# Reading the token operand of a matmul as two halves in turns, and moving the phases of its operands

## The chip, the cores and the metric

The kernel runs on one core of one Trainium2 chip. A core has five engines with instruction streams of their own (TensorE for matmuls, VectorE, ScalarE, GpSimd, SyncE), an on-chip memory of 128 partitions (SBUF), an accumulator memory for matmul outputs (PSUM) and DMA queues to the device memory. The metric is the device time of one execution in microseconds. Before the change it is 2859.04 us, the median of three runs (2858.79 to 2860.81).

In the profile PE is TensorE's matmul stream, PEld its weight loads, DVE is VectorE, ACT is ScalarE, POOL is GpSimd and SP is SyncE. A name like L184 is a line of the kernel's file.

## What is computed

One layer of a decoder over 280 tokens: 16 learned meta tokens, 256 prompt tokens and 8 sample tokens, with a model width of 2048 and an inner width of 5504, all in fp32:

```python
x = layer_norm(ALPHA * x + 0.5 * swiglu(x, f1_g, f1_u, f1_d), ln1_g, ln1_b)
m, s_ret, s_hg = token_mixer(x, ...)     # 10 projections of x, two recurrences, w_out
x = layer_norm(ALPHA * x + m, ln2_g, ln2_b)
x = layer_norm(ALPHA * x + 0.5 * swiglu(x, f2_g, f2_u, f2_d), ln3_g, ln3_b)

def swiglu(x, w_gate, w_up, w_down):
    return (jax.nn.silu(x @ w_gate) * (x @ w_up)) @ w_down
```

Outputs are the tokens without the meta tokens and the recurrent states. Each weight matrix is read once; nearly all arithmetic is in the dense products.

## The kernel before

**Layout.** Features lie on partitions, tokens along the free axis. The 2048 features are 16 tiles of 128 (`KC`), the inner 5504 are 43 (`FC`). A dense product is a sequence of matmuls with a 128x128 weight block as stationary operand and one token tile of 280 columns (264 from the output gate on: the meta tokens are dropped) as moving operand.

**Two parts for each number.** Weights and tokens are split into a high and a low part (`whi`, `wlo`; `xh`, `xl`; `hh`, `hl` for the inner activations; `yh`, `yl` for the mixer's output). Each block takes three matmuls into the same PSUM bank: high by high (L183), high weights by low tokens (L184), low weights by high tokens (L185). These three lines, in `dense`, are nearly all of TensorE's work. Each matmul has its own weight load, which overlaps the matmul before it.

**Order of the dense work.** The up product (names `up...`) goes by 22 groups of two inner tiles, gate and up for each, so four output banks: for each of the 16 token tiles `k`, four blocks in turn, hence 16 x 4 x 3 = 192 matmuls a group (96 in the last). The down product (`dn...`) goes by 16 output tiles, each summed over 43 inner tiles, one bank at a time. The mixer (`pj_...`) projects in groups of two with 16 token tiles each, and between its matmuls, by `pump`, the recurrences run as generators. The output projection (`wo`) follows. The first group of the mixer and of the second up product is made by `Norm.first`, from token tiles (`xhg`, `xlg`) that have not been normalised yet and are two columns wider; then `Norm.normalise` writes the final tiles. TensorE's order is the order of the program; the other engines' work is ordered by the scheduler, with weight loading at high priority.

**Weight feed.** `stream` loads 8 blocks (a unit, 512 KB) by one DMA from SyncE's queue into `raw` (three buffers). ScalarE casts it to `whi` (L157) and VectorE subtracts to get `wlo` (L158), three buffers each. A unit feeds 24 matmuls.

**Where the operands lie.** SBUF addresses are bytes within a partition. `raw` has a pitch of 512 bytes per block; `whi` and `wlo` are padded to `WP` = 132 columns per block, a pitch of 528 bytes, so successive blocks start 16 bytes further modulo 512, and a buffer is 4224 bytes. The token tiles `xh` and `xl` are separate tiles of `XP` = 296 columns (1184 bytes) of which a window of 280 or 264 is used; `x_tiles` shifts its start by 0 to 12 columns by the tile's number. `hh` and `hl` are tiles of exactly 280 or 264 columns (1120 or 1056 bytes).

Of the kernel before, what the change touches and what calls it, by code (L numbers as in the profile page):

```python
# [11 lines left out]
F32R = mybir.dt.float32r  # L12
# [6 lines left out]
P = 128  # L19
D = 2048  # L20
KC = D // P
DFF = 5504
FC = DFF // P
NMETA, SEQ, NS = 16, 256, 8
LP = NMETA + SEQ
T = LP + NS
# [5 lines left out]
U = 8  # L32


WP = P + 4
XP = 296

WARM = 7

# [14 lines left out]
def ffn_up_groups():  # L54
    g = []
    for m in range(0, FC, 2):
        ms = list(range(m, min(m + 2, FC)))
        g.append([("g", x) for x in ms] + [("u", x) for x in ms])
    return g
# [42 lines left out]
def trunk(ctx: ExitStack, tc: tile.TileContext, A, O):  # L102
    nc = tc.nc
    cst = ctx.enter_context(tc.tile_pool(name="cst", bufs=1))
    xp = ctx.enter_context(tc.tile_pool(name="xp", bufs=1))
    rp = ctx.enter_context(tc.tile_pool(name="rp", bufs=1))
    wp = ctx.enter_context(tc.tile_pool(name="wp", bufs=3))
# [5 lines left out]
    def acc_bank(name):  # L113
        return ps_a.tile([P, 512], F32, tag="acc", name=name)
# [25 lines left out]
    def turn(n):  # L140

        return tc.high_priority(offset=tc.tile_snap_priority() + 100 * (9 - n))

    def stream(w_dram, at_once=False):

        n_units = w_dram.shape[0]
        state = {"u": -1, "j": U, "hi": None, "lo": None}

        def load(u, parts=((0, U, tc.high_priority),)):
            raw = wp.tile([P, U, P], F32, tag="raw", name=f"raw{u}", bufs=3)  # L150
            hi = wp.tile([P, U, WP], F32R, tag="whi", name=f"whi{u}")[:, :, :P]
            lo = wp.tile([P, U, WP], F32R, tag="wlo", name=f"wlo{u}")[:, :, :P]
            src = w_dram[u].rearrange("p (b c) -> p b c", b=U)
            for j0, j1, when in parts:
                with when():
                    nc.sync.dma_start(raw[:, j0:j1, :], src[:, j0:j1, :])
                    nc.scalar.copy(hi[:, j0:j1, :], raw[:, j0:j1, :])  # L157
                    nc.vector.tensor_tensor(out=lo[:, j0:j1, :], in0=raw[:, j0:j1, :], in1=hi[:, j0:j1, :].bitcast(F32), op=ALU.subtract)  # L158
            return hi, lo

        def block():
            if state["j"] == U:
                state["u"] += 1
                assert state["u"] < n_units
                state["hi"], state["lo"] = load(state["u"])
                state["j"] = 0
            j = state["j"]
            state["j"] += 1
            return state["hi"][:, j, :], state["lo"][:, j, :]

        if at_once:
            state["hi"], state["lo"] = load(0, ((0, 2, lambda: turn(1)), (2, U, lambda: turn(2))))
            state["u"] = state["j"] = 0
        return block

    def dense(block, nk, outs, xhi, xlo, cols=slice(0, T), hook=None):
        n = len(outs)
        for k in range(nk):
            for i in range(n):
                wh, wl = block()  # L180
                h, l = xhi[k][:, cols], xlo[k][:, cols]
                o = outs[i][:, : h.shape[1]]
                nc.tensor.matmul(o, wh, h, start=k == 0, stop=False)  # L183
                nc.tensor.matmul(o, wh, l, start=False, stop=False)  # L184
                nc.tensor.matmul(o, wl, h, start=False, stop=k == nk - 1)  # L185
            if hook is not None:
                hook(k)

    def split(hi, lo, x):
        nc.scalar.copy(hi, x)  # L190
        nc.vector.tensor_tensor(out=lo, in0=x, in1=hi.bitcast(F32), op=ALU.subtract)  # L191
# [6 lines left out]
    def mul(out, a, b):  # L198
        nc.vector.tensor_tensor(out=out, in0=a, in1=b, op=ALU.mult)
# [20 lines left out]
    xh = [None] * KC  # L220
    xl = [None] * KC

    def x_tiles(c, which, n=T):
        for e, (x, nm) in enumerate(((xh, "xh"), (xl, "xl"))):
            o = 4 * ((2 * c + e) // 8 % 2) + 8 * (c % 2) * e
            x[c] = xp.tile([P, XP], F32R, tag=f"{nm}{c}", name=f"{nm}{which}_{c}")[:, o : o + n]

    def row_tile(name, n=T):
        return rp.tile([P, n], F32, tag=name, name=name)
# [1 line left out]
    class Norm:  # L231
# [57 lines left out]
        def shifted(self, m):  # L289
            n, d = self.n, self.d[m]  # L290
            if m == 0:
                nc.scalar.copy(self.s1, d)
                nc.scalar.activation(self.s2, d, AF.Square)
            else:
                self.q = q = self.row("lnq")
                nc.scalar.activation(q, d, AF.Square)
                if m == KC - 1 and not self.lead:
                    return
                add(self.s1, self.s1, d)
                add(self.s2, self.s2, q)  # L300
            if self.lead:
                x_tiles(m, f"g{self.which}", n + 2)
                g = self.g[:, m : m + 1]
                dx = self.dx[m][:, : n + 1]
                nc.scalar.activation(xh[m][:, : n + 1], dx, AF.Identity, scale=g)
                nc.vector.scalar_tensor_tensor(
                    out=xl[m][:, : n + 1], in0=dx, scalar=g, in1=xh[m][:, : n + 1].bitcast(F32), op0=ALU.mult, op1=ALU.subtract)
                nc.vector.tensor_copy(xh[m][:, n + 1 : n + 2], self.bs[:, 0, m : m + 1])
                nc.vector.tensor_copy(xl[m][:, n + 1 : n + 2], self.bs[:, 1, m : m + 1])
# [34 lines left out]
        def normalise(self):  # L344
            for c in range(KC):
                d = self.d[c]
                g, b = self.g[:, c : c + 1], self.b[:, c : c + 1]
                sub(d, d, self.mean)
                nc.vector.scalar_tensor_tensor(out=d, in0=d, scalar=g, in1=self.r, op0=ALU.mult, op1=ALU.mult)
                x_tiles(c, self.which, self.n)  # L350
                nc.scalar.activation(xh[c], d, AF.Identity, bias=b)  # L351
                nc.vector.scalar_tensor_tensor(  # L352
                    out=xl[c], in0=d, scalar=b, in1=xh[c].bitcast(F32), op0=ALU.add, op1=ALU.subtract)
# [37 lines left out]
    def ffn(i, block, w_dn, which, before=None):  # L391

        n = T if before is None else TL
        cols = slice(0, n)
        with tc.tile_pool(name=f"h{i}", bufs=1) as hp:
            hh, hl = [None] * FC, [None] * FC
            for gn, grp in enumerate(ffn_up_groups()):
                bank = acc_bank if gn % 2 == 0 else mx_bank
                outs = [bank(f"up{gn}_{j}") for j in range(len(grp))]
                if gn == 0 and before is not None:  # L400
                    outs = before.first(block, outs)
                else:
                    dense(block, KC, outs, xh, xl, cols)
                ng = len(grp) // 2
                for j in range(ng):
                    m = grp[j][1]
                    sg = hp.tile([P, n], F32, tag="sg", name=f"sg{m}", bufs=2)
                    nc.scalar.activation(sg, outs[j][:, :n], AF.Silu)
                    mul(sg, sg, outs[ng + j][:, :n])
                    hh[m] = hp.tile([P, n], F32R, tag=f"hh{m}", name=f"hh{m}")  # L410
                    hl[m] = hp.tile([P, n], F32R, tag=f"hl{m}", name=f"hl{m}")
                    split(hh[m], hl[m], sg)
            if before is not None:

                warm = hp.tile([P, 1], F32, tag="warm", name="warm")
                nc.scalar.activation(warm, sg[:, 0:1], AF.Abs_reciprocal_sqrt, scale=0.0, bias=eps_l)
            block = stream(w_dn)
            norm = Norm(which, n, False, i == 1)
            for m in range(KC):
                o = acc_bank(f"dn{m}")  # L420
                norm.ahead(m)
                dense(block, FC, [o], hh, hl, cols, (lambda k: k == 6 and norm.shift()) if m == 1 else None)
                norm.chunk(m, o[:, :n])
        return norm


    with tc.tile_pool(name="inp", bufs=2) as ip:
# [11 lines left out]
        up1 = stream(A["w_up1"], at_once=True)  # L439
# [19 lines left out]
    nc.sync.dma_start(sel, A["sel"])  # L459

    norm1 = ffn(1, up1, A["w_dn1"], 1)


    with tc.tile_pool(name="yp", bufs=1) as yp:
        yh, yl = [None] * KC, [None] * KC
        with tc.tile_pool(name="mp", bufs=1) as mp:
# [25 lines left out]
            nc.sync.dma_start(sin, A["sin"])  # L492

            block = stream(A["w_in"])
            st = {}
            on_r, on_h = {}, {}
# [375 lines left out]
        block = stream(A["w_out"])  # L872
        norm2 = Norm(2, TL, True, True)
        for gn, grp in enumerate(out_groups()):
            outs = [acc_bank(f"wo{m}") for m in grp]
# [4 lines left out]


    norm3 = ffn(2, stream(A["w_up2"]), A["w_dn2"], 3, norm2)
    norm3.finish(O["y"])

# [111 lines left out]
```

## Time and profile before

| | value |
|---|---|
| median of three runs | 2859.04 us |
| the profiled execution's span, first to last instruction | 2857.5 us |
| TensorE matmul (PE) busy | 2829.5 us, 99% |
| TensorE weight load (PEld) busy | 2775.9 us, 97% |
| VectorE busy | 1688.2 us, 59% |
| ScalarE busy | 1328.4 us, 46% |
| granted TensorE clock, mean | 0.999 |
| DMA | 186 GB/s from and to device memory over the span |

The profile shows of the profiled execution its span; no other time of it is given, and the runs' median lies 1.5 us above that span. The dense stages follow one another: first up product until about 543 us, first down product until about 809 us, the mixer until about 1993 us, the output projection until about 2087 us, second up product until about 2588 us, second down product until about 2841 us, then the last normalisation and the output.

How to read the rows: in the rows of groups, "x" is a count; after the bar stand busy time, mean duration of one, and the idle time of the engine before them with what ended it. Rows of one tile's instructions have shortest, median and longest duration in ns, then the first and last start in us. Matmuls are pipelined: a matmul's duration is longer than the distance to the next one's start, so the pace is busy time by count, or the distance between starts.

### The profile page before, as it was taken

The numbers are of one execution on the slowest core, as the hardware profiler recorded it, in microseconds if no ns is written. First come the engines' busy times: TensorE is split into PE (matmuls) and PEld (weight loads), VectorE is DVE, ScalarE is ACT, GpSimd is POOL, SyncE is SP. The second block draws the span as 40 slices with busy tenths as digits, with TensorE's granted clock in tenths as the row PEclk, the third lists the DMA queues.
The fourth block names the chain that finished last, engine by engine and source line by source line (L and its number), as shares of the span: only waits on it lengthen the run. The fifth ranks groups of instructions, "written<-read, shape, count | busy, mean of one in ns | idle before, by whom it ended". The sixth has DMA issues, their size and how long they took to land.

```text
span 2857.5 us, 54281 instructions
## 1 busy us (share of the span) xinstructions
PE 2829.5 (99%) x22704; PEld 2775.9 (97%) x22704; DVE 1688.2 (59%) x2677; ACT 1328.4 (46%) x1931; POOL 3.4 (0%) x38
## 2 busy tenths in 40 slices
PE   9999999999999999999999999999999999999999
PEld 8999999999999999999999998999999999999998
DVE  5444444555477767676767676666884444446444
ACT  4333334433354564545555554545454444444333
POOL 0000000000000000000000000000000000000000
PEclk9999999999999999999999999999999999999999
DMA  6555555455556665656565656565555555555554
GB/s 219 171 170 170 170 171 170 169 172 171 171 187 205 208 225 192 218 197 218 196 218 194 227 178 230 178 219 166 180 177 179 184 181 182 183 180 180 181 178 141
DMA packets 154438, 536.27 MB, mean 188 GB/s; under 512 B 17808, under 2 KB 25936, under 8 KB 154192
## 3 DMA queue, kind: packets, MB, share of 16 engines
q1 hardware_dynamic: 154048, 532.65, 55.8%
q8 instruction: 178, 2.92, 0.4%
q14 instruction: 68, 0.56, 0.1%
q10 hardware_dynamic: 144, 0.14, 0.0%
HBM read 502.12 MB, written 30.61 MB: 186 GB/s over the span
## 4 chain that ended last, share of the span: by engine, by line
PE 94%; DMA 2%; ACT 2%; DVE 1%; issue 1%; SPq 0%; ACTq 0%; DVEq 0%
PE up L184 12%; PE up L185 12%; PE up L183 12%; PE dn L183 6%; PE dn L184 6%; PE dn L185 6%; PE pj_v_r L183 1%; DMA smr<-in_sr 1%; PE pj_g_r L183 1%; PE pj_k_r L183 1%; PE pj_v_r L184 1%; PE pj_k_r L184 1%; PE pj_k_r L185 1%; PE pj_v_r L185 1%; PE wo L183 1%; PE pj_f L183 1%
## 5 line engine op out<-in xcount | busy, mean ns | idle before, releaser
L158 DVE TENSOR_TENSOR wlo<-raw,whi 128x1024 fp32r<-128x1024 f32 (+1 forms) x869 | 1063.5, 1224 | 916.7 <-ACT whi L157 912.5
L157 ACT CAST whi<-raw 128x1024 fp32r<-128x1024 f32 (+1 forms) x869 | 909.7, 1047 | 1159.8 <-PE up L184 484.2
L183 PE MATMUL up<-xh,whi 128*128 128x280 f32 (+1 forms) x2688 | 772.3, 287 | 3.3 <-ACT xh L190 2.4
L185 PE MATMUL up<-xh,wlo 128*128 128x280 f32 (+1 forms) x2688 | 773.1, 288 | 1.2 <-DVE wlo L158 1.2
L184 PE MATMUL up<-xl,whi 128*128 128x280 f32 (+1 forms) x2688 | 773.4, 288 | 0.1
L183 PEld LDWEIGHTS up<-xh,whi 128*128 128x128 f32 x2688 | 505.8, 188 | 4.0 <-ACT xh L190 2.6
L185 PEld LDWEIGHTS up<-xh,wlo 128*128 128x128 f32 x2688 | 505.8, 188 | 1.8 <-DVE wlo L158 1.7
L184 PEld LDWEIGHTS up<-xl,whi 128*128 128x128 f32 x2688 | 505.5, 188 | 0.3 <-DVE xl L191 0.3
L183 PE MATMUL dn<-hh,whi 128*128 128x280 f32 (+1 forms) x1376 | 397.1, 289 | 0.0
L184 PE MATMUL dn<-hl,whi 128*128 128x280 f32 (+1 forms) x1376 | 395.8, 288 | 0.0
L185 PE MATMUL dn<-hh,wlo 128*128 128x280 f32 (+1 forms) x1376 | 395.7, 288 | 0.0
L184 PEld LDWEIGHTS dn<-hl,whi 128*128 128x128 f32 x1376 | 259.0, 188 | 0.1
L183 PEld LDWEIGHTS dn<-hh,whi 128*128 128x128 f32 x1376 | 258.9, 188 | 0.1
L185 PEld LDWEIGHTS dn<-hh,wlo 128*128 128x128 f32 x1376 | 258.6, 188 | 0.0
L183 PE MATMUL pj_g_r<-xh,whi 128*128 128x264 f32 x256 | 81.9, 320 | 0.0
L184 PE MATMUL pj_i_h<-xl,whi 128*128 128x280 f32 x256 | 74.9, 293 | 2.9 <-DVE xl L352 2.9
L183 PE MATMUL pj_g_h<-xh,whi 128*128 128x264 f32 x256 | 77.4, 302 | 0.0
L183 PE MATMUL pj_v_r<-xh,whi 128*128 128x280 f32 x256 | 76.0, 297 | 0.0
L183 PE MATMUL pj_k_r<-xh,whi 128*128 128x280 f32 x256 | 75.9, 297 | 0.0
L183 PE MATMUL pj_i_h<-xh,whi 128*128 128x280 f32 x256 | 75.0, 293 | 0.7 <-ACT xh L351 0.7
L184 PE MATMUL pj_v_r<-xl,whi 128*128 128x280 f32 x256 | 74.7, 292 | 0.0
L184 PE MATMUL pj_k_r<-xl,whi 128*128 128x280 f32 x256 | 74.6, 291 | 0.0
(337 smaller groups left out, 5169.4 us busy)
## 6 DMA issues: line engine op xcount, KB each, us to landing
raw<-in_w_up SPq DMA_DIRECT2D x343, 512.0 KB, 3.5
raw<-in_w_in SPq DMA_DIRECT2D x320, 512.0 KB, 3.6
raw<-in_w_dn SPq DMA_DIRECT2D x172, 512.0 KB, 3.5
smr<-in_sr SPq DMA_DIRECT2D x32, 512.0 KB, 6.1
out_srs<-smr SPq DMA_DIRECT2D x32, 512.0 KB, 4.0
raw<-in_w_out SPq DMA_DIRECT2D x32, 512.0 KB, 3.5
smh<-in_sg SPq DMA_DIRECT2D x16, 512.0 KB, 4.0
out_sgs<-smh SPq DMA_DIRECT2D x16, 512.0 KB, 6.1
```

The costliest lines, as they stand in the source:

```text
L157: nc.scalar.copy(hi[:, j0:j1, :], raw[:, j0:j1, :])
L158: nc.vector.tensor_tensor(out=lo[:, j0:j1, :], in0=raw[:, j0:j1, :], in1=hi[:, j0:j1, :].bitcast(F32), op=ALU.subtract)
L183: nc.tensor.matmul(o, wh, h, start=k == 0, stop=False)
L184: nc.tensor.matmul(o, wh, l, start=False, stop=False)
L185: nc.tensor.matmul(o, wl, h, start=False, stop=k == nk - 1)
```

## The change

Three things are edited.

In `dense`, the moving operand and the output can be read in another order. `lines` takes the free axis as two halves (`a`), each cut into pieces of 4 columns (`i`, 16 bytes), and lets the order run over the pieces first and the halves second: piece 0 of the first half, piece 0 of the second, piece 1 of the first, and so on. The same columns go to the same places of the output. This is on in three stages, `SPLIT`: both up products and the second down product. It is off in the first down product, the mixer, the output projection and the first groups that `Norm.first` makes. With 280 columns a half is 140 columns (560 bytes, 512 + 48), with 264 it is 132 (528 bytes, 512 + 16).

The weight blocks lose their padding: `whi` and `wlo` have a pitch of 512 bytes, and a buffer 4096.

The high and low token tiles of one feature tile become one tile of `XW` = 616 columns (2464 bytes), with the low part `XLO` = 320 columns (1280 bytes) after the high one; tiles 8 to 15 start `LINE` = 4 columns (16 bytes) further.

```diff
-WP = P + 4
-XP = 296
+XLO = 320
+XW = 616
+LINE = 4
+SPLIT = {"up1", "up2", "dn2"}
...
+    def lines(ap, on):
+
+        return ap.rearrange("p (a l i) -> p l a i", a=2, i=LINE) if on else ap
+
...
-            hi = wp.tile([P, U, WP], F32R, tag="whi", name=f"whi{u}")[:, :, :P]
-            lo = wp.tile([P, U, WP], F32R, tag="wlo", name=f"wlo{u}")[:, :, :P]
+            hi = wp.tile([P, U, P], F32R, tag="whi", name=f"whi{u}")
+            lo = wp.tile([P, U, P], F32R, tag="wlo", name=f"wlo{u}")
...
-    def dense(block, nk, outs, xhi, xlo, cols=slice(0, T), hook=None):
+    def dense(block, nk, outs, xhi, xlo, cols=slice(0, T), hook=None, split_lines=False):
...
-                h, l = xhi[k][:, cols], xlo[k][:, cols]
-                o = outs[i][:, : h.shape[1]]
+                h, l = (lines(x[k][:, cols], split_lines) for x in (xhi, xlo))
+                o = lines(outs[i][:, : cols.stop - cols.start], split_lines)
                 nc.tensor.matmul(o, wh, h, start=k == 0, stop=False)
...
     def x_tiles(c, which, n=T):
-        for e, (x, nm) in enumerate(((xh, "xh"), (xl, "xl"))):
-            o = 4 * ((2 * c + e) // 8 % 2) + 8 * (c % 2) * e
-            x[c] = xp.tile([P, XP], F32R, tag=f"{nm}{c}", name=f"{nm}{which}_{c}")[:, o : o + n]
+        t = xp.tile([P, XW], F32R, tag=f"x{c}", name=f"x{which}_{c}")
+        o = LINE * (c // 8)
+        xh[c], xl[c] = t[:, o : o + n], t[:, XLO + o : XLO + o + n]
...
-                    dense(block, KC, outs, xh, xl, cols)
+                    dense(block, KC, outs, xh, xl, cols, None, f"up{i}" in SPLIT)
...
-                dense(block, FC, [o], hh, hl, cols, (lambda k: k == 6 and norm.shift()) if m == 1 else None)
+                dense(block, FC, [o], hh, hl, cols, (lambda k: k == 6 and norm.shift()) if m == 1 else None, f"dn{i}" in SPLIT)
```

## The prediction

> **What bounds the kernel now.** I read the page's engine totals first, then the chain that ended last, then the busy time by stage.
>
> ```profile
> span 2857.5 us, 54281 instructions
> PE 2829.5 (99%) x22704; PEld 2775.9 (97%) x22704; DVE 1688.2 (59%) x2677; ACT 1328.4 (46%) x1931; POOL 3.4 (0%) x38
> ...
> PE 94%; DMA 2%; ACT 2%; DVE 1%; issue 1%; SPq 0%; ACTq 0%; DVEq 0%
> ```
>
> TensorE is busy for 99% of the span and is 94% of the chain. The next view cuts the span into stages: first up product, first down product, the mixer, the output projection, second up product, second down product. Its columns are busy time and count per engine, the granted clock, the DMA share and GB/s.
>
> ```profile
> core 0: us, PE busy (x) PEld busy (x) DVE busy (x) ACT busy (x) POOL busy (x), PEclk, DMA share, GB/s
> 20.00:540.00 520.00, 517.49 (x4015) 517.08 (x4014) 242.60 (x266) 209.95 (x263) 0.00 (x0) 1.00 0.52 174
> 545.00:805.00 260.00, 260.00 (x2018) 259.91 (x2018) 140.18 (x207) 100.55 (x116) 0.00 (x0) 1.00 0.51 171
> 815.00:1990.00 1175.00, 1157.85 (x9411) 1108.73 (x9410) 803.48 (x1500) 625.24 (x1050) 1.18 (x12) 1.00 0.61 204
> 1993.00:2086.00 93.00, 92.86 (x759) 92.54 (x758) 73.76 (x159) 45.62 (x66) 0.39 (x4) 1.00 0.52 179
> 2113.00:2586.00 473.00, 473.00 (x3911) 473.00 (x3910) 242.41 (x281) 204.76 (x259) 0.00 (x0) 1.00 0.55 182
> 2590.00:2838.00 248.00, 248.00 (x2034) 247.94 (x2033) 130.01 (x160) 94.29 (x102) 0.00 (x0) 1.00 0.54 173
> ```
>
> In the three stages that the change splits (rows 1, 5 and 6) TensorE has almost no idle time and the full clock, so the time is a number of matmuls times a pace. The pace is busy time by count: 517.49/4015 = 128.9 ns in the first up product, 473.00/3911 = 120.9 ns in the second, 248.00/2034 = 121.9 ns in the second down product. No instruction is removed, so only this pace can move much.
>
> **What the pace is made of.** The next rows give shortest, median and longest duration of one matmul: up and down product, first half (280 columns) and second half (264).
>
> ```profile
> L185 PE MATMUL up<-xh,wlo x1338: 285/291/304, 19.9 to 539.7; 128*128 128x280 f32 x192
> L184 PE MATMUL dn<-hl,whi x672: 285/291/297, 544.9 to 804.7; 128*128 128x280 f32 x168
> L184 PE MATMUL up<-xl,whi x1304: 278/283/293, 2112.7 to 2585.9; 128*128 128x264 f32 x187
> L184 PE MATMUL dn<-hl,whi x677: 278/284/296, 2589.9 to 2837.7; 128*128 128x264 f32 x170
> ```
>
> The shortest durations differ by 7 ns for 16 columns, 0.44 ns a column. The median lies 5 to 6 ns above the shortest, the longest 12 to 19. That this is no noise shows in two stretches of the first up product, 74.20 us apart; columns are start and duration.
>
> ```profile
> 164.79 0.28 PE L185 MATMUL up<-xh,wlo 128*128 128x280 f32 x1
> 164.92 0.29 PE L183 MATMUL up<-xh,whi 128*128 128x280 f32 x1
> 165.04 0.30 PE L184 MATMUL up<-xl,whi 128*128 128x280 f32 x1
> 165.18 0.29 PE L185 MATMUL up<-xh,wlo 128*128 128x280 f32 x1
> ...
> 238.99 0.28 PE L185 MATMUL up<-xh,wlo 128*128 128x280 f32 x1
> 239.12 0.29 PE L183 MATMUL up<-xh,whi 128*128 128x280 f32 x1
> 239.25 0.30 PE L184 MATMUL up<-xl,whi 128*128 128x280 f32 x1
> 239.38 0.29 PE L185 MATMUL up<-xh,wlo 128*128 128x280 f32 x1
> ```
>
> 74.20 us is three output groups of 192 matmuls, and 24 weight units, a multiple of the three buffers: at equal places the two stretches have the same token tiles and weight buffers, so the same addresses. The same matmul is fast (0.28) and the same one slow (0.30, then 0.14 to the next start) both times. What makes matmuls unequal is thus a matter of addresses. Other engines and DMA do not repeat on that beat. I read it as the token stream and the weight load of the next matmul getting in each other's way.
>
> [...]
>
> **The change, part by part.**
>
> *Tokens in two halves in turns.* It reaches 4128 matmuls of the first up product, 3936 of the second (its first group reads whole) and 2064 of the second down product: 10128. Columns and count stay; the order goes 4 columns (16 bytes) of the first half, 4 of the second, and so on, on the read and on the output. The trace holds no output written so. It does hold reads in pieces: the small score matmuls read 64 columns in pieces of 4 at 874.60 and of 16 at 885.67.
>
> ```profile
> 874.60 1.00 PE L656 MATMUL pl<-Q,K 128*128 128x64 f32 x8
> 875.40 0.37 PE L183 MATMUL pj_k_r<-xh,whi 128*128 128x280 f32 x1
> ...
> 885.67 1.00 PE L656 MATMUL pl<-Q,K 128*128 128x64 f32 x8
> 886.48 0.38 PE L183 MATMUL pj_v_r<-xh,whi 128*128 128x280 f32 x1
> ```
>
> From eight of them to the next matmul pass 0.80 and 0.81 us: 16-byte pieces cost the read nothing there, at about 1.6 ns a column, a slower stream than ours.
>
> What the order does to the meeting of the streams follows from their speeds.
>
> ```profile
> L184 PEld LDWEIGHTS up<-xl,whi 128*128 128x128 f32 x2688 | 505.5, 188 | 0.3 <-DVE xl L191 0.3
> L825 PEld LDWEIGHTS pqr<-smr,qdr 128*32 128x32 f32 x256 | 6.9, 112 | 5.4 <-issue 0.6 <-DVE gt L585 0.2
> ```
>
> A weight load takes (188 - 112)/96 = 0.79 ns a column: 3.2 ns per 16 bytes, 101 ns for a block's 512. Tokens go at 0.44 ns a column, 1.75 ns per 16 bytes: now they run through the addresses nearly twice as fast as the weights and pass them, modulo 512, in nearly every matmul. Read in turns, each half advances 16 bytes in 3.5 ns, within a tenth of the weights' 3.2. The distance then hardly changes during a matmul: a half that starts clear stays clear, one that starts on top stays near.
>
> Price, both ends. Best, every split matmul at its shortest: 6 ns in the first up product (291 - 285), 5 in the second (283 - 278), 6 in the second down product (284 - 278): 4128 x 6 + 3936 x 5 + 2064 x 6 = 24.8 + 19.7 + 12.4 = 56.9 us less. Worst, every one at its longest: 304 - 291 = 13 ns, 293 - 283 = 10, 296 - 284 = 12: 53.7 + 39.4 + 24.8 = 117.9 us more. I take half of the gain, -28.4 us: two half streams at 32 token places against one weight place must leave some pairs near each other, and nothing in the trace says how near is too near.
>
> *Weight blocks at one phase, token tiles at many.* Block pitch goes from 528 to 512 bytes, so all blocks of all buffers start at one place modulo 512 (buffers are 4096 bytes). A joint token tile is 2464 bytes (4 x 512 + 416), its low part 1280 bytes in, and from tile 8 on 16 bytes further: the 32 starts fall on 32 different 16-byte places of 512, where before they fell on 12. This reaches the other dense matmuls too, about 10700 with the groups that read whole, whose order stays plain. Their price: medians of like matmuls at different tiles lie 291 to 292 (280 columns) and
>
> ```profile
> L183 PE MATMUL pj_q_h<-xh,whi x224: 278/283/390, 917.4 to 1823.9; 128*128 128x264 f32 x112
> L185 PE MATMUL pj_g_h<-xh,wlo x256: 280/285/291, 1018.9 to 1992.0; 128*128 128x264 f32 x128
> L183 PE MATMUL pj_f<-xh,whi x224: 285/291/396, 897.1 to 1812.2; 128*128 128x280 f32 x112
> L184 PE MATMUL pj_f<-xl,whi x224: 287/292/297, 897.3 to 1812.4; 128*128 128x280 f32 x112
> ```
>
> 283 to 285 (264), so +-1 ns: +-10.7 us. I take 0: plain streams still sweep past the weights from every start, and averages over places move less than single places.
>
> *What else moves.* The cast and the subtraction that fill the blocks write 1024 columns in one run, not eight.
>
> ```profile
> L158 DVE TENSOR_TENSOR wlo<-raw,whi 128x1024 fp32r<-128x1024 f32 (+1 forms) x869 | 1063.5, 1224 | 916.7 <-ACT whi L157 912.5
> L157 ACT CAST whi<-raw 128x1024 fp32r<-128x1024 f32 (+1 forms) x869 | 909.7, 1047 | 1159.8 <-PE up L184 484.2
> ...
> raw<-in_w_up SPq DMA_DIRECT2D x343, 512.0 KB, 3.5
> ```
>
> Any change there is 0 while the weight feed is covered. A unit of 8 blocks feeds 24 matmuls: 24 x 120.9 = 2.90 us, or 2.78 with the full 5 ns gain. Per unit ScalarE casts for 1.05 us and VectorE subtracts for 1.22, both in the shadow, and ScalarE waits for TensorE to free a buffer (484.2 us), not the reverse. The load lands in 3.5 us with three raw buffers, so it has some 8 us. At the split stages' DMA share of 0.52 to 0.55, a 5% faster pace needs 0.58. If that cover went, a unit would cost 3.5 us, 0.6 more than now; I see no sign of it. High and low tokens now share a tile, so a write of one may wait for readers of the other; both are read by the same three matmuls of a block, one pace (0.12 us) apart, at two stage edges of 16 tiles: at most 32 x 0.12 = 4 us, and 0 is taken, because VectorE fills the low part after the high anyway.
>
> **Sum.** The profiled execution's span is 2857.5 us, 1.5 below the 2859.0 median of the runs. 2857.5 - 28.4 + 1.5 = 2830.6 us.
>
> **The rivals.**
>
> *All of it goes* (0.18). If only exact meetings hurt and few starts meet, the pace falls to the shortest: 2859.0 - 56.9 = 2802 us. For: equal speeds make meetings rare. Against: speeds are 3.5 and 3.2, a drift of about three places per matmul, so near starts still meet.
>
> *Nothing moves* (0.12). If a meeting costs as much met once in passing as held, or the 5 to 6 ns come from elsewhere in the address, the mean stays: 2859 +- 4. For: in all five stages, with different tile pitches, the median sits at the same 5 to 6 ns. Against: single matmuls differ by more than that.
>
> *Standing collisions: slower* (0.18). Place: split matmuls whose half starts near the weights; they hold the collision for the whole sweep and run at the longest duration, 117.9 us/10128 = 11.6 ns over the median, while the others gain 56.9/10128 = 5.6. It decides from a share s with 11.6 s = 5.6 (1 - s), s = 0.33; at a half, 10128 x (5.8 - 2.8) = +30 us: 2889. For: two halves, one weight phase, and starts on every place, so none can be avoided. If within one place counts, two halves hit 6 of 32 starts, a share of 0.19; if the pattern repeats every 256 bytes, 0.38, over the point. Against: a stalled stream falls behind and is then clear.
>
> *The output in pieces: slower* (0.06). If each of the 66 or 70 jumps of the output costs one column (0.44 ns), a matmul grows by about 30 ns: 10128 x 30 = +304 us, 3163. The traces bear out nothing for it; the score matmuls write their output whole. [...]
>
> **How the numbers follow.** Half the gain (0.46): 2831, its own range 2815 to 2850. With "all of it" faster has 0.64; "nothing" is the 0.12 within 0.2% (5.7 us, about what a measurement of this kernel can tell from no change); the two slower rivals make 0.24. The low end takes the full gain and 5 us of the plain stages: 2797. The high end cuts the collisions at 2872; beyond it and below 2797 lie 2 in 10.
>
> **What would show it right or wrong.** Right: up and second down medians 2 to 4 ns nearer to shortest, pace near 126 and 118 ns, first down product and mixer within 1 ns, ScalarE still waiting for TensorE. The forecast is wrong if the split stages' medians stay at 291 and 283 (nothing moves), if some tiles run near 300 throughout and others at 285 (collisions), if shortest durations rise by tens (output), or if TensorE begins to wait for weights.

## The result and the profile after

The changed kernel takes 2939.05 us (median of 4 runs, 2935.30 to 2943.95) against 2859.93 us for the kernel before (4 runs): ratio 1.0273, 95% interval 1.0259 to 1.0288. It is 79 us slower, where 28 us less was forecast.

From the page of the changed kernel: the span, the engines, and the groups that answer to the casts and the weight feed before.

```profile
span 2935.7 us, 54282 instructions
PE 2910.3 (99%) x22704; PEld 2856.9 (97%) x22704; DVE 1689.8 (58%) x2677; ACT 1337.6 (46%) x1931; POOL 3.4 (0%) x38
...
L164 DVE TENSOR_TENSOR wlo<-raw,whi 128x1024 fp32r<-128x1024 f32 (+1 forms) x869 | 1063.1, 1223 | 984.8 <-ACT whi L163 980.9
L163 ACT CAST whi<-raw 128x1024 fp32r<-128x1024 f32 (+1 forms) x869 | 916.3, 1054 | 1227.6 <-PE up L190 526.9
```

The counts of all engines are those of before. TensorE's busy time grew by 80.8 us, the span by 78.2; VectorE and ScalarE did nearly the same work and waited longer, ScalarE still for TensorE (526.9 us, 484.2 before). So TensorE itself became slower, and no wait took its place. Where, is in the busy time by stage of the changed kernel (first up, first down, mixer, output projection, second up, second down; columns as in the prediction).

```profile
20.00:560.00 540.00, 537.58 (x4019) 537.32 (x4019) 243.09 (x267) 211.17 (x263) 0.00 (x0) 1.00 0.52 167
565.00:822.00 257.00, 257.00 (x2002) 256.91 (x2001) 138.80 (x205) 100.27 (x116) 0.00 (x0) 1.00 0.54 171
840.00:2005.00 1165.00, 1149.13 (x9324) 1100.13 (x9323) 796.22 (x1487) 619.80 (x1042) 1.19 (x12) 1.00 0.62 203
2010.00:2105.00 95.00, 94.87 (x777) 94.52 (x776) 74.74 (x159) 47.05 (x68) 0.40 (x4) 1.00 0.57 179
2140.00:2640.00 500.00, 500.00 (x3822) 500.00 (x3821) 234.76 (x267) 202.29 (x247) 0.00 (x0) 1.00 0.53 168
2650.00:2910.00 260.00, 260.00 (x1978) 259.94 (x1977) 128.12 (x157) 95.78 (x100) 0.00 (x0) 1.00 0.52 164
```

Busy time by count gives the pace:

| stage | columns | before, ns | after, ns | matmuls | us |
|---|---|---|---|---|---|
| first up, in turns | 280 | 128.9 | 133.8 | 4128 | +20 |
| first down, plain | 280 | 128.8 | 128.4 | 2064 | -1 |
| second up, in turns | 264 | 120.9 | 130.8 | 3936 | +39 |
| second down, in turns | 264 | 121.9 | 131.4 | 2064 | +20 |

The three stages make +79 us, all of the difference. Clock and DMA share stayed (clock 1.00 in each stage; DMA 0.51 to 0.61 before, 0.52 to 0.62 after). With 264 columns the loss is twice that with 280 (9.9 and 9.5 ns a matmul against 4.9). The rows of single matmuls in the changed kernel (shortest, median, longest duration in ns; first up and second up product) show that even the best case is gone:

```profile
L190 PE MATMUL up<-x,whi x1339: 293/299/438, 22.9 to 559.6; 128*128 128x280 f32 x192
L189 PE MATMUL up<-x,whi x1274: 287/294/307, 2139.7 to 2639.7; 128*128 128x264 f32 x182
```

The shortest is 293 and 287 ns, where it was 285 and 278, and the median 299 and 294, where it was 291 and 283. The forecast took half of a gain between median and shortest; instead the shortest and the median moved together.

### The profile page after: what moved, and what is told of

It reads as the page before. It is cut to its first block, busy times and chain, and to the rows that moved or that the text cites. A ratio compares the mean times of both kernels' runs of the same rounds, so it can differ in the third digit from the quotient of the medians.

```text
span 2935.7 us, 54282 instructions
## 1 busy us (share of the span) xinstructions
PE 2910.3 (99%) x22704; PEld 2856.9 (97%) x22704; DVE 1689.8 (58%) x2677; ACT 1337.6 (46%) x1931; POOL 3.4 (0%) x38
## 4 chain that ended last, share of the span: by engine, by line
PE 95%; ACT 2%; DMA 2%; DVE 1%; issue 0%; SPq 0%; ACTq 0%; DVEq 0%
PE up L190 12%; PE up L191 12%; PE up L189 12%; PE dn L189 6%; PE dn L190 6%; PE dn L191 6%; PE pj_v_r L189 1%; PE pj_g_r L189 1%; PE pj_f L189 1%; PE pj_k_r L189 1%; PE pj_g_h L189 1%; PE pj_v_r L190 1%; PE pj_v_r L191 1%; PE pj_k_r L190 1%; PE pj_f L190 1%; PE pj_f L191 1%
## 5 line engine op out<-in xcount | busy, mean ns | idle before, releaser
L163 ACT CAST whi<-raw 128x1024 fp32r<-128x1024 f32 (+1 forms) x869 | 916.3, 1054 | 1227.6 <-PE up L190 526.9
L189 PE MATMUL up<-x,whi 128*128 128x280 f32 (+1 forms) x2688 | 798.5, 297 | 2.4 <-ACT x L196 2.3
L191 PE MATMUL up<-x,wlo 128*128 128x280 f32 (+1 forms) x2688 | 798.2, 297 | 0.7 <-DVE wlo L164 0.7
L190 PE MATMUL up<-x,whi 128*128 128x280 f32 (+1 forms) x2688 | 798.8, 297 | 0.1
L189 PEld LDWEIGHTS up<-x,whi 128*128 128x128 f32 x2688 | 510.4, 190 | 3.0 <-ACT x L196 2.6
L191 PEld LDWEIGHTS up<-x,wlo 128*128 128x128 f32 x2688 | 510.0, 190 | 1.2 <-DVE wlo L164 1.2
L190 PEld LDWEIGHTS up<-x,whi 128*128 128x128 f32 x2688 | 510.6, 190 | 0.3 <-DVE x L197 0.3
L189 PE MATMUL pj_g_r<-x,whi 128*128 128x264 f32 x256 | 82.0, 320 | 0.0
L189 PE MATMUL pj_g_h<-x,whi 128*128 128x264 f32 x256 | 77.5, 303 | 0.0
L189 PE MATMUL pj_i_h<-x,whi 128*128 128x280 f32 x256 | 75.9, 296 | 1.6 <-ACT f L543 0.8
L190 PE MATMUL pj_i_h<-x,whi 128*128 128x280 f32 x256 | 75.3, 294 | 2.0 <-DVE x L358 2.0
L189 PE MATMUL pj_v_r<-x,whi 128*128 128x280 f32 x256 | 76.3, 298 | 0.0
L189 PE MATMUL pj_k_r<-x,whi 128*128 128x280 f32 x256 | 75.8, 296 | 0.0
L191 PE MATMUL pj_i_h<-x,wlo 128*128 128x280 f32 x256 | 75.2, 294 | 0.0
L190 PE MATMUL pj_v_r<-x,whi 128*128 128x280 f32 x256 | 74.7, 292 | 0.0
```

## The experiments

Three theories were put up. W: a token half stands near the weight load that runs beside it, and stays there, because both now advance at the same speed. R: the order of the token read costs by itself, without the weights; as R1 by where the next piece lies, as R2 by a fixed price for each jump. O: the output written in pieces costs.

**1. The layout alone.**

```diff
-SPLIT = {"up1", "up2", "dn2"}
+SPLIT = set()
```

> Only the layout part of the change: weight blocks at one phase, joint token tiles, no reading in turns anywhere. Theory W (standing meetings of token halves and weight load), theory R (the order of the read costs by itself) and theory O (the output in pieces costs) all put the loss on the split, so all expect about 2860 us, within 10 us of the kernel before. A result near 2939 us would say that the layout alone is the cause and would end all three.

Measured: 2860.43 us against 2862.98 in the same job, ratio 0.9989, interval 0.9978 to 1.0001. The interval holds 1: the phases of weight blocks and token tiles are worth nothing that can be told from zero, and the loss belongs to the reading or writing in turns. Its stages (second up, second down):

```profile
2125.00:2588.00 463.00, 463.00 (x3819) 463.00 (x3818) 230.90 (x259) 198.08 (x247) 0.00 (x0) 1.00 0.58 181
2594.00:2838.00 244.00, 244.00 (x2005) 243.93 (x2004) 128.93 (x158) 92.06 (x99) 0.00 (x0) 1.00 0.56 175
```

**2. Reading and writing in turns on the layout of before.** The kernel before, with `lines` and its calls as in the change, and nothing else of it:

```diff
+LINE = 4
+SPLIT = {"up1", "up2", "dn2"}
...
-                h, l = xhi[k][:, cols], xlo[k][:, cols]
-                o = outs[i][:, : h.shape[1]]
+                h, l = (lines(x[k][:, cols], split_lines) for x in (xhi, xlo))
+                o = lines(outs[i][:, : cols.stop - cols.start], split_lines)
```

> Only the reading and writing in turns, on the kernel-before's padded weight blocks and separate token tiles. W: the weight blocks stand at many places, so the distance of the streams differs from block to block; with the starts on all places the share of meetings stays about the same, so about 2939 us, but the pace varies inside a weight unit, which it did not do with the single phase. R and O: the loss belongs to the order and not to the phases, so about 2939 us within 10 us, with a pace that goes by the token tile alone (R) or by nothing (O).

Measured: 2940.66 us, one run, with 133.8, 131.3 and 131.3 ns in the three stages. The loss is the same without the new phases. W does not fall by the mean, which it expected too. Its other sign is missing: averaged by place in the weight unit of 24 matmuls (second up product, starts in the traces), the pace runs from 128.5 to 133.6 ns here and from 128.6 to 134.1 in the changed kernel, so it varies no more with the blocks at many places.

**3 and 4. Only the read, only the write.** In the changed kernel one of the two operands is left in one run.

```diff
-                o = lines(outs[i][:, : cols.stop - cols.start], split_lines)
+                o = outs[i][:, : cols.stop - cols.start]
```

> The changed kernel with the token operand still read in turns, but the output written in one run: the columns of the split products therefore hold the tokens in another order, and the result is not the reference's. Same instructions and counts. W and R: the loss stays, about 2939 us within 10 us. O: the loss goes, about 2860 us.

```diff
-                h, l = (lines(x[k][:, cols], split_lines) for x in (xhi, xlo))
+                h, l = xhi[k][:, cols], xlo[k][:, cols]
```

> The changed kernel with the token operand read in one run and the output written in turns of 16 bytes; the split products' columns hold the tokens in another order, so the result is not the reference's. O: the loss stays, about 2939 us. W and R: the loss goes, about 2860 us within 10 us.

Measured, one run each: 2933.80 us with the read alone, 2863.36 us with the write alone (before, in the same job: 2862.98, 13 runs from 2855.54 to 2868.97). The busy time by stage (second up, second down) of the kernel that only reads in turns:

```profile
2140.00:2640.00 500.00, 500.00 (x3820) 500.00 (x3820) 232.33 (x260) 201.86 (x247) 0.00 (x0) 1.00 0.53 168
2650.00:2910.00 260.00, 260.00 (x1978) 259.94 (x1977) 128.12 (x157) 94.90 (x99) 0.00 (x0) 1.00 0.51 162
```

and of the one that only writes in turns:

```profile
2125.00:2590.00 465.00, 465.00 (x3835) 465.00 (x3835) 233.93 (x265) 199.20 (x248) 0.00 (x0) 1.00 0.57 182
2596.00:2840.00 244.00, 244.00 (x2005) 243.93 (x2004) 128.95 (x158) 93.24 (x100) 0.00 (x0) 1.00 0.55 175
```

130.9 and 131.4 ns for the read, 121.3 and 121.7 for the write, 121.2 and 121.7 in the same stages of study 1, which does neither. O is dead: an output in pieces of 16 bytes, alternating between two places, costs nothing here that these paces show.

**5. The orders by themselves.** A kernel without the layer: after loading one weight unit and some tokens it runs 256 matmuls for each way of reading, with the output in one run.

```python
for name, view, n, m in runs:                 # m: columns of the weight block
    o = ps_a.tile([P, 512], F32, tag="acc", name=name)
    for r in range(8):
        for q in range(32):
            x = view(LINE * (q * (2 * r + 1) % 32))   # token start
            nc.tensor.matmul(out, wt[:, (q + r) % U, :m], x, ...)
```

`apart` reads two halves that lie a given number of lines (16 bytes) apart, `parts` several parts of one run in turns, `piece` two halves in pieces of other sizes, `narrow` has weight blocks of 32 columns.

> Not the layer: 256 matmuls each of 38 ways to read the token operand, back to back on TensorE, each with its own 128x128 weight load, weight blocks at one phase, token starts on all 32 places of 512 bytes in mixed orders; all outputs are zeros. No other engine works. Theory W (a half that stands near the weight load): the pace of two halves is about 131 ns with 264 columns and 133 with 280 at every distance between the halves, since all starts occur at each; with weight loads of 32 columns instead of 128 the loss shrinks to a quarter (2 to 3 ns); reading all even pieces and then all odd ones, which sweeps faster and not slower, costs nothing over the plain read (121). Theory R1 (the two halves get in each other's way): the pace goes with the distance of the halves, near the plain 121 and 128 ns at some distances and above 131 at others, with a period; the loss stays with narrow weights. Theory R2 (each jump of the read costs by itself): the same 131 and 133 at every distance, and with narrow weights too; pieces of 48 bytes a third of the loss (124), of 176 bytes a tenth (122).

Rows of this kernel. The pace is the time from first to last start by 255; it is worked out here, and in studies 6 and 9, from the starts in the trace, which are whole ns (the rows round them to 0.1 us, which is 0.4 ns a matmul). In order: halves 33, 36 and 48 lines apart, six parts, twenty-two parts (264 columns); pieces of 8 bytes; narrow plain, narrow halves 33 apart; plain and halves 35 apart with 280 columns.

```profile
L178 PE MATMUL apartSa<-xt,wt x256: 288/295/308, 72.6 to 106.1; 128*128 128x264 f32 x128
L178 PE MATMUL apartSd<-xt,wt x256: 285/289/296, 170.8 to 202.8; 128*128 128x264 f32 x128
L178 PE MATMUL apartSp<-xt,wt x256: 288/296/308, 559.1 to 592.8; 128*128 128x264 f32 x128
L178 PE MATMUL partsSb<-xt,wt x256: 282/287/294, 941.5 to 973.0; 128*128 128x264 f32 x128
L178 PE MATMUL partsSd<-xt,wt x256: 277/282/291, 1015.1 to 1045.6; 128*128 128x264 f32 x128
L178 PE MATMUL pieceSc<-xt,wt x256: 333/338/344, 1205.3 to 1248.6; 128*128 128x264 f32 x128
L178 PE MATMUL narrowplain<-xt,wt x256: 278/283/289, 1248.8 to 1279.4; 128*32 128x264 f32 x128
L178 PE MATMUL narrowsplit<-xt,wt x256: 287/293/304, 1279.5 to 1312.6; 128*32 128x264 f32 x128
L178 PE MATMUL plainL<-xt,wt x256: 285/291/303, 39.6 to 72.4; 128*128 128x280 f32 x128
L178 PE MATMUL apartLa<-xt,wt x256: 294/297/302, 626.5 to 660.5; 128*128 128x280 f32 x128
```

- With no other engine at work the layer's numbers come back: halves 33 lines apart 131.5 ns (131 in the layer), halves 35 apart with 280 columns 133.4 (133.8 in the layer), plain with 280 columns 128.8 (128.9), plain with 264 columns 121.8 (in the rows of study 6; 120.9 and 121.9 in the layer).
- Narrow weights keep the loss: 129.5 against 120.2 ns, 9.3 more, where wide ones have 9.7. W expected 2 to 3. W falls.
- The distance of the halves counts: 36 apart 125.4 ns; 48 apart 132.2. Of the 17 distances from 33 to 49, the three that are 0 or 1 modulo 16 lines (33, 48, 49) cost 131.3 to 132.2 ns, the other 14 cost 125.4 to 127.4. R2, with one price for every jump, falls; twenty-two parts, with as many jumps as the halves, refute it too: 119.7 ns, below the plain read.
- R1 missed as well: it expected some distances near the plain pace, and none is. With 264 columns every pair of halves loses 3.6 ns or more; with 280 columns seven of eight distances cost 132.8 to 134.2 ns, the 35 of the change among them, and 48 costs 139.7.
- Pieces of 8 bytes, halves 33 apart, cost 169.9 ns; longer ones cost less than 131.5, 127.6 with 48 bytes and 123.6 with 176.

**6. More orders.** The same kernel with other views: `parts` with other numbers, halves with pieces of 48 and 176 bytes.

```diff
+    runs += [("strideS" + A_Z[k], parts(a, 264), 264, P) for k, a in ((2, 33), (3, 22), (11, 6), (22, 3))]
+    runs += [("strideL" + A_Z[k], parts(a, 280), 280, P) for k, a in ((2, 35), (5, 14), (7, 10), (10, 7), (14, 5))]
+    runs += [("nearS" + A_Z[k], apart(48, 264, i), 264, P) for k, i in enumerate((4, 12, 44))]
...
+    runs += [("pairL" + A_Z[k], pairs(a, 280, 8), 280, P) for k, a in enumerate((5, 7))]
...
```

`pairs` is `parts` with pieces of 8 columns, two lines.

> Not the layer, as in the study of orders before: 256 matmuls for each way of reading, all outputs zeros. Theory R1 (what counts is how far the next 16-byte piece lies from the one just read, modulo 256 bytes): strides of 2 and 3 lines again at or below the plain pace (121.5 and 119.7 ns), 11 lines about 123.4, 22 about 156, with the narrow weights as with the wide ones; for 280 columns strides of 5, 7, 10, 14 lines spread widely, and 14 (2 below 16) is among the worst; with halves a multiple of 256 bytes apart the loss of 10 ns falls with the number of jumps, to about 4 at pieces of 48 bytes. Theory R2 (a fixed price for each jump whatever its length): all strides with the same number of jumps cost the same, about 126 for 264 columns and 133 for 280.

Rows of this kernel: parts 3 lines apart, plain, halves 48 lines apart in pieces of 16 and of 48 bytes, seven parts of 280 columns in pieces of 32 bytes.

```profile
L184 PE MATMUL strideSd<-xt,wt x256: 277/282/291, 134.7 to 165.1; 128*128 128x264 f32 x128
L184 PE MATMUL againS<-xt,wt x256: 278/284/295, 864.1 to 895.1; 128*128 128x264 f32 x128
L184 PE MATMUL nearSa<-xt,wt x256: 288/296/310, 503.7 to 537.4; 128*128 128x264 f32 x128
L184 PE MATMUL nearSb<-xt,wt x256: 279/285/295, 537.5 to 568.7; 128*128 128x264 f32 x128
L184 PE MATMUL pairLb<-xt,wt x256: 300/307/309, 797.1 to 833.0; 128*128 128x280 f32 x128
```

119.5 ns for the parts against 121.8 plain; the halves fall from 132.2 to 122.3 with pieces three lines long, a loss of under 1 ns where about 4 was expected. (Longer pieces change the jumps as well as their number: with 16 bytes they go 48 lines on and 47 back, with 48 bytes 46 on and 47 back.) Two expectations missed, this one and the next: with 280 columns a step of 14 lines came out among the best (129.9 ns from start to start on average, plain 128.8) and not among the worst; 5, 7 and 10 cost 135 to 138. The last row goes one line on and nine on in turns and costs 140.9. Three parts, so 22 lines on, cost 156.2 ns with wide weights and 156.3 with narrow ones.

**7. Six parts in the layer.**

```diff
-        return ap.rearrange("p (a l i) -> p l a i", a=2, i=LINE) if on else ap
+        return ap.rearrange("p (a l i) -> p l a i", a=6 if ap.shape[1] == TL else 2, i=LINE) if on else ap
```

> The changed kernel, but in the second up and second down product the tokens are read as six parts of 44 columns in turns (the next piece 11 lines of 16 bytes on) and not as two halves (33 lines on, 1 modulo 16). Same number of jumps, same layout, same result. R1: these 6000 matmuls fall from 131 to about 123.5 ns, -45 us: about 2893 us. R2, and W of before: 66 jumps as ever, about 2939 us.

Measured: 2894.62 us, R1's 2893 within 2 us. The stages of this kernel (second up, second down):

```profile
2140.00:2620.00 480.00, 480.00 (x3892) 480.00 (x3891) 239.84 (x277) 203.24 (x254) 0.00 (x0) 1.00 0.56 178
2625.00:2872.00 247.00, 247.00 (x2011) 246.93 (x2011) 128.96 (x158) 93.01 (x100) 0.00 (x0) 1.00 0.55 173
```

123.3 and 122.8 ns: the same number of jumps, and against the kernel before the loss goes from 10 to 2.4 and 0.9 ns with the place of the next piece.

**8. Three lines on, wherever there are 264 columns.**

```diff
-SPLIT = {"up1", "up2", "dn2"}
+PARTS = {264: 22}
...
-        return ap.rearrange("p (a l i) -> p l a i", a=2, i=LINE) if on else ap
+        return ap.rearrange("p (a l i) -> p l a i", a=PARTS[n], i=LINE) if n in PARTS else ap
...
```

> The changed kernel's layout, no halves; every product of 264 columns (second up and down product, six of the ten projections, output projection, about 11100 matmuls) reads and writes its tokens as 22 parts of 12 columns in turns, so that the next piece lies 3 lines of 16 bytes on; 280 columns are read in one run. R1 with the pace of 119.7 against 121.6 ns: about -21 us against reading in one run, 2840 us, a gain of 0.7%. R2: 66 jumps cost as in the halves, about 9 ns a matmul, +100 us: 2960 us.

Measured: 2843.27 us (6 runs) against 2863.05 for the kernel before in the same job (11 runs), ratio 0.9925, interval 0.9911 to 0.9939: shorter than both kernels, by 0.7% to 0.8% where 0.7% was expected. Against the layout alone (2860.43 us, study 1) it is 17 us, where 21 were expected. Its stages (second up, second down):

```profile
2110.00:2570.00 460.00, 460.00 (x3849) 460.00 (x3849) 237.11 (x273) 200.81 (x252) 0.00 (x0) 1.00 0.59 184
2580.00:2820.00 240.00, 240.00 (x2005) 239.93 (x2004) 128.59 (x158) 91.96 (x99) 0.00 (x0) 1.00 0.55 178
```

119.5 and 119.7 ns, against 120.9 and 121.9 before.

**9. One step at a time.** The kernel of orders again, with one even step from each piece to the next, through a longer token tile with holes:

```python
def step(d, n):          # pieces of 4 columns, d lines apart
    k = n // LINE
    return lambda s: xt[:, s : s + k * LINE * d].rearrange("p (l c) -> p l c", c=LINE * d)[:, :, :LINE]
```

> Not the layer: 256 matmuls for each step from 1 to 36 lines of 16 bytes between successive pieces of the token read (264 columns, 66 pieces, a longer tile with holes, output in one run), some also with 280 columns and with 32-column weight loads; all outputs are zeros. Theory R1, with the period of 256 bytes that the halves showed: the pace repeats when the step grows by 16 (1, 17 and 33 near 121.5; 3 and 19 near 119.5; 6 and 22 far above, over 150); steps of 16 and 32, which stay on one place, are the worst or near it; the same steps are dear with narrow weights and with 280 columns. If instead the length of the step counts and not its place modulo 256 bytes, the pace rises with the step and does not repeat. If the weight load were the partner after all (W), narrow weights would be within 3 ns of plain at every step.

Rows of this kernel: steps of 1 (plain), 3, 5, 6, 13, 16, then 17, 19, 22 and 32 lines; step 6 with narrow weights; step 3 with 280 columns.

```profile
L186 PE MATMUL plainS<-xt,wt x256: 278/284/295, 39.6 to 70.7; 128*128 128x264 f32 x128
L186 PE MATMUL stepac<-xt,wt x256: 277/282/290, 166.0 to 196.6; 128*128 128x264 f32 x128
L186 PE MATMUL stepae<-xt,wt x256: 300/304/312, 228.0 to 263.3; 128*128 128x264 f32 x128
L186 PE MATMUL stepaf<-xt,wt x256: 332/337/340, 263.5 to 305.9; 128*128 128x264 f32 x128
L186 PE MATMUL stepam<-xt,wt x256: 302/304/312, 498.6 to 534.1; 128*128 128x264 f32 x128
L186 PE MATMUL stepap<-xt,wt x256: 310/314/323, 596.9 to 635.0; 128*128 128x264 f32 x128
L186 PE MATMUL stepaq<-xt,wt x256: 278/284/295, 635.1 to 666.2; 128*128 128x264 f32 x128
L186 PE MATMUL stepas<-xt,wt x256: 278/282/290, 697.4 to 728.0; 128*128 128x264 f32 x128
L186 PE MATMUL stepav<-xt,wt x256: 332/337/340, 794.8 to 837.2; 128*128 128x264 f32 x128
L186 PE MATMUL stepbf<-xt,wt x256: 310/314/323, 1128.3 to 1166.3; 128*128 128x264 f32 x128
L186 PE MATMUL narrowf<-xt,wt x256: 326/343/346, 1531.0 to 1573.4; 128*32 128x264 f32 x128
L186 PE MATMUL stepLc<-xt,wt x256: 284/289/298, 1323.6 to 1356.0; 128*128 128x280 f32 x128
```

The pace repeats with 16 lines, 256 bytes, to 0.1 ns: 1 and 17 at 121.7 and 121.8, 3 and 19 both at 120.2, 6 and 22 both at 166.3, 16 and 32 both at 149.1. All 36 steps do. The means over all token starts, by step modulo 16:

| step | 0 | 1 | 2 | 3 | 4 | 5 | 6 | 7 | 8 | 9 | 10 | 11 | 12 | 13 | 14 | 15 |
|---|---|---|---|---|---|---|---|---|---|---|---|---|---|---|---|---|
| ns | 149.1 | 121.7 | 121.3 | 120.2 | 122.0 | 138.6 | 166.3 | 123.9 | 129.8 | 122.2 | 130.5 | 122.6 | 123.2 | 139.2 | 123.3 | 121.7 |

Narrow weights leave step 6 at 166.2 and step 16 at 148.7; step 8 rises from 129.8 to 134.0. A step of 16 lines, which always comes back to the same place, is not the worst but the second; 6 is. Step 3 is the best of the five tried with 280 columns too: 127.2 ns against 128.8 plain; step 14 costs 130.6 there.

## Why the prediction was wrong, step by step

*What bounds the kernel.* Right: TensorE's pace in the three split stages is all that moved, the weight feed stayed covered and the plain stages moved by less than 0.5 ns.

*What the pace is made of.* The prediction read the 5 to 6 ns between shortest and median as the token stream and the weight load in each other's way, and so as a gain to be had. The narrow weights bound that: with a load of 32 columns instead of 128 the plain pace was 120.2 ns (study 5) against 121.8 (study 6), 1.6 less. Most of the 5 to 6 ns is not the weight load's. One premise was wrong: other engines do repeat on the beat of 74.20 us. ScalarE's cast beside the first stretch comes again beside the second (start and duration in us, kernel before):

```profile
165.42 1.05 ACT L157 CAST whi<-raw 128x1024 fp32r<-128x1024 f32 x1 [2.03 <-PE up L184]
239.62 1.05 ACT L157 CAST whi<-raw 128x1024 fp32r<-128x1024 f32 x1 [2.03 <-PE up L184]
```

So the two stretches alone could not tell addresses from other engines. The kernel of orders can: with no other engine at work the plain read has the same spread, 278/284/295 with 264 columns. Two runs of it, in studies 6 and 9, agree matmul by matmul (correlation 0.97 over 255 distances between starts). So addresses do make single matmuls unequal, but by itself that says nothing of the partner. With 32-column loads and the same token starts other matmuls are the slow ones (correlation -0.09 with the wide read of study 9), so the weight load may have a part in which matmul is slow; in the mean it is worth the 1.6 ns. The partner was not found.

*Tokens in two halves in turns: the step that failed.* The sum had -28.4 us here; the runs have +79. Two sentences broke. The first is that pieces of 16 bytes cost the read nothing: the score matmuls that it rests on read every second piece at 874.60, a step of 2 lines, which is one of the cheap ones (121.3 ns), and stream slowly besides, at about 1.6 ns a column. The price of pieces goes by where the next piece lies, and no row of before held the order of the change: 33 lines on and 32 back (1 and 0 modulo 16) with 264 columns, 35 on and 34 back (3 and 14) with 280. The second is the argument from equal speeds. It ran on the distance between tokens and weights modulo 512 bytes, and that this distance counts was the author's assumption; the runs show a cost of the token read by itself, which is there with weight loads a quarter as wide (9.3 ns against 9.7). Sized by the orders alone: 131.5 against 121.8 ns, 9.7, for 6000 matmuls, and 133.4 against 128.8, 4.6, for 4128: 58 + 19 = 77 us of the 79.

How far the single step explains this differs. With 264 columns one jump in two stays on its place modulo 256 bytes, a step that is dear alone (149.1 ns), and most halves at other distances lose 4 to 6 ns in place of 9.7. With 280 columns it explains nothing: 3 and 14 cost 127.2 and 130.6 ns alone, 128.9 on average, which is the plain pace, and the pair costs 133.4. That part of the loss, 19 us, is shown to come from the order of the read, not why.

*The ends of the range.* The bound above, every matmul at its longest (+117.9 us, 10 to 13 ns a matmul), held by luck: it came from the spread of plain reads, and an order with step 6 would have cost over 44 ns a matmul (166.3 against 121.8). The range was cut at 2872 on the ground that a stalled stream gets clear by itself, which no run shows, and the chance beyond it was put too low.

*The layout.* Right in its size: 0 was taken; -0.1% was measured, with an interval that holds zero.

*The rivals.* "Standing collisions" had the side, but neither the size (+30 us) nor the partner: the loss stays with narrow weights (9.3 ns) and changes with the distance of the halves (125.4 to 132.2 ns with 264 columns). "The output in pieces" is refuted by the write alone, which came out 0.4 us from the kernel before, far less than runs of one kernel differ.

**What stays open.** Prices of even steps do not add up when steps take turns. Halves 36 lines apart go 4 on and 35 back (4 and 13 modulo 16), which alone cost 122.0 and 139.2 ns, and the pair takes 125.4. Steps of 1 and 9 in turns, each at the plain pace alone (264 columns), cost 140.9 with 280 columns, 12 over plain. Why 6 is dearer than 0, and why all halves in pieces of 16 bytes cost about 4 ns or more, was not found either.

## What to carry to other kernels

When a matmul's moving operand is read in pieces of 16 bytes, ask where each next piece lies. With one even step the pace went by that step modulo 256 bytes: with 264 columns, steps of 0, 5, 6, 8, 10 and 13 lines of 16 bytes were dear (129.8 to 166.3 ns), 1 to 4 cheap (120.2 to 122.0), and a step of 3 was faster than reading straight on (120.2 against 121.7). With steps that take turns, as in two halves, these prices did not foretell the pace (4 and 13, alone 122.0 and 139.2 ns, took 125.4 together). A row that shows an access to be free shows it for its own order alone, so before such an order is put into a kernel, run a few hundred matmuls of it by themselves: here that gave the pace in the layer to within a nanosecond.

## What was not expected of the hardware

- With one even step between pieces of 16 bytes, the pace of a matmul went by that step with a period of 256 bytes over the 36 steps tried, from 120.2 to 166.3 ns for the same 264 columns.
- Reading 48 bytes on each time beat the plain read, 119.5 against 121.8 ns, and made the whole layer about 0.7% faster.
- An output that alternates between two places every 16 bytes cost nothing that can be told: 2863.36 us against 2862.98.
- Two halves read in turns in pieces of 16 bytes cost 3.6 ns or more over the plain read at every distance tried, also where both steps are cheap alone.
- Halving the piece to 8 bytes, with the halves 33 lines apart, took the pace from 131.5 to 169.9 ns.
